# A diffusion transformer layer on one core: LayerNorm 1's scalars re-ranked, one room for two column sums, the last Newton steps on ScalarE

## The chip, the cores and the metric

One core of a Trainium2 chip runs the whole program. The time is device microseconds of one launch, from the core's first instruction to its last, with the launch's own small part around it. Before the change three executions took 1171.78, 1173.62 and 1175.6 us; the median is 1173.62 us. One more execution was profiled, and all views come from that one.

The engines are named as in the profile: PE (TensorE, the matrix products; PEld are its weight loads), DVE (VectorE), ACT (ScalarE), POOL (GpSimd) and SP (SyncE, whose queue issues all the loads here).

## What is computed

One layer with an adaptive modulation: six vectors (shift, scale and gate, twice) come from a conditioning vector; attention over 256 latent and 256 context tokens; an output projection; a gated residual; a LayerNorm; a modulated SwiGLU feed-forward part; a gated residual; a second LayerNorm. Everything is float32, D = 2048 columns, 5632 hidden columns.

```python
def layer_norm(x, g, b):
    xf = x.astype(jnp.float32)
    mu = jnp.mean(xf, axis=-1, keepdims=True)
    var = jnp.mean(jnp.square(xf - mu), axis=-1, keepdims=True)
    return ((xf - mu) * lax.rsqrt(var + EPS) * g + b).astype(x.dtype)
...
        sh1, sc1, g1, sh2, sc2, g2 = ada_mods(c, w_ada[layer], b_ada[layer])
...
        x = layer_norm(DN_ALPHA * x + g1 * (heads @ w_out[layer]), ln1_g[layer], ln1_b[layer])

        x = layer_norm(DN_ALPHA * x + g2 * swiglu(modulate(x, sh2, sc2), w_gate[layer], w_up[layer], w_down[layer]),
                       ln2_g[layer], ln2_b[layer])
```

## The kernel before

The 256 tokens are two tiles of 128 rows, t = 0 and 1. Every large product is done in three passes (`mm3`, lines 223 to 226): a float32 operand is split into a high part, cast by ACT (`hi`, L214 or L446), and a low part, the difference, by DVE (`lo`, L215 or L449); PE then adds hi by hi, lo by hi and hi by lo. A weight block of 512 x 512 is one load of 1 MB into a `raw` buffer (four of them), two ACT casts and two DVE casts of 128 x 1024 each, and 24 products of 512 columns (four slices of 128 rows, two tiles, three passes). The raw buffer is free again after its second DVE cast; there are four rooms for pairs of hi and lo.

The work runs in stages: the modulated input and its projection, attention, the output projection with the gated residual, LayerNorm 1, the first half of the gate and up products (`first_half`), the rest of the feed-forward part, the down projection, LayerNorm 2 and the store.

Up to LayerNorm 1 the order of the instructions on all five engines is written by a planner in the kernel, the class `Flow`. Each step is added with an engine, a duration in nanoseconds, the steps it comes after, the rooms it takes and gives, and a rank (`F.at`, in planned microseconds; smaller goes first among the steps that are ready). `Flow.run` plays the plan and issues the steps in the order that comes out. A step becomes ready some time after its forerunner ends: `SAME` on the same engine, `OTHER` across engines. END, the planned end of attention, is the base of the ranks around LayerNorm 1.

The output projection takes its column blocks n = 0 to 3 (`flow_out`, 512 columns each). The last one is done tile by tile: all products of tile 0, then all of tile 1. Behind each block DVE multiplies by the gate (L1035), adds to the residual (L1038, L1041) and takes statistics (`bn_stats`, L1044). When the four blocks of a tile are through, `ln_scalars(t)` (L969 to L979) makes mean and 1/sqrt(var + eps): an aggregation, four small steps that set up a start value from the bits of the variance, and three Newton rounds of two steps. `normalise(n, t)` (L986) then subtracts and scales 512 columns. `scalars(t)` (L1226 on) is `ln_scalars` with `normalise` of block 0.

Behind the planner the order is still as written until `region.__exit__`, and the compiler's scheduler places the rest. `z_flip` (L1233) transposes two column slices of a tile on PE; `z_rest` (L1338 to L1341) modulates them on ACT and splits them into `u2h` and `u2l`; `first_products(i, t)` are the twelve products of a tile with the first block of w_gate (i = 0) or w_up (i = 1). Before the change the written order is: z_rest of tile 0, scalars of tile 1, gate products of tile 0, z_flip of tile 1, up products of tile 0, z_rest of tile 1, then all products of tile 1, then the six late `normalise`.

The modulation of the feed-forward part needs, for each of four column groups, a sum over w_ada. Group 1's shift is summed by PE (`m1_sums`, L1200: 16 products into `bank1`), copied by ACT into `adav1` and turned into columns by four small products (`second_shifts`, L1213). Group 1's scale is summed by DVE (L332, sixteen steps over four loads of 1 MB; `scales`, an `ada_vector_steps`), into a room that POOL zeroes first (L309) and to which a short bias load goes (L315); `second_scales` (L1221) makes columns of it. `vector_sums` gives the one room with the tag `adav`; `late_sums[1]` gives a different one, with the tag `lgb`. Groups 2 and 3 (`side`) follow in the same way, summing shift and scale together, in `adav` and `lgb`. The scale steps are merged with three weight blocks of `first_half`.

At the end, behind the last block of the down projection, DVE does per tile the residual (L962, L963), the statistics (L964), `ln_scalars`, four steps that subtract the mean and multiply by g (L1447) and four that multiply by 1/sigma and add b (L1448), each followed by a store.

Of the kernel before, what the change touches and what calls it, by code (L numbers as in the profile page):

```python
# [12 lines left out]
F32 = mybir.dt.float32  # L13
F32R = mybir.dt.float32r
BF16 = mybir.dt.bfloat16
I32 = mybir.dt.int32
ET = mybir.EngineType
AF = mybir.ActivationFunctionType
ALU = mybir.AluOpType
# [3 lines left out]
P = 128  # L23
D = 2048
# [11 lines left out]
NB = 512  # L36
# [29 lines left out]
class Flow:  # L66
# [1 line left out]


    ENGINES = ("SP", "PE", "ACT", "DVE", "POOL")  # L70
    SAME = {"SP": 0, "PE": 0, "ACT": 60, "DVE": 80, "POOL": 80}
    OTHER = {"SP": 2000, "PE": 270, "ACT": 90, "DVE": 90, "POOL": 150}

    PATIENCE = 0
# [75 lines left out]
def dit_layer(ctx: ExitStack, tc: tile.TileContext, x, c, cx, c_ctx, w_ada, b_ada, w_in, q_norm_g,  # L150
              k_norm_g, sink_logit, w_out, ln1_g, ln1_b, w_gate, w_up, w_down, ln2_g, ln2_b,
              rope_cos, rope_sin, out):
    nc = tc.nc
# [134 lines left out]
    def ada_vector_steps(starts, width, sums, done):  # L288


        st = {}
        ns = len(starts)
        w = ns * width
        nk = G4 * NB // w

        def step(g):
            if g == 0:
                st["a"] = first_sums(sums(), starts, width)
            raw = raw_tile()
            vector_load(raw, starts, width, g)  # L300
            for i in range(G4 * NB // min(w, 2 * NB)):
                vector_sum(raw, st["a"], w, g, i)
            if g == KD // nk - 1:
                done(st["a"])

        return [lambda g=g: step(g) for g in range(KD // nk)]
# [29 lines left out]
    def vector_sums(width):  # L336
        return main.tile([P, 2 * NB], F32, tag="adav", name="adav")[:, :width]
# [625 lines left out]
        nc.vector.tensor_add(base[:, t, sl], base[:, t, sl], y)  # L963
        nc.vector.bn_stats(stats[:, t, n, :], base[:, t, sl])  # L964

    def ln_scalars(t):

        mv = main.tile([P, 2], F32, tag="mv", name="mv", bufs=2)
        nc.vector.bn_aggr(mv, stats[:, t, :, :])  # L969
        v = main.tile([P, 2], F32, tag="lv", name="lv", bufs=2)  # L970
        y = main.tile([P, 1], F32, tag="ly", name="ly", bufs=2)
        a = main.tile([P, 1], F32, tag="la", name="la", bufs=2)
        nc.vector.tensor_scalar_add(v[:, 0:1], mv[:, 1:2], EPS)
        nc.vector.tensor_single_scalar(a.bitcast(I32), v[:, 0:1].bitcast(I32), 1, op=ALU.logical_shift_right)
        nc.vector.tensor_scalar_mul(v[:, 1:2], v[:, 0:1], -0.5)
        nc.vector.tensor_scalar(y.bitcast(I32), a.bitcast(I32), -1.0, float(0x5F3759DF), op0=ALU.mult, op1=ALU.add)
        for _ in range(3):
            nc.vector.tensor_scalar(a, y, y, v[:, 1:2], op0=ALU.mult, op1=ALU.mult)
            nc.vector.tensor_scalar(y, a, 1.5, y, op0=ALU.add, op1=ALU.mult)  # L979
        return mv[:, 0:1], y  # L980

    norm = {}

    def normalise(n, t):
# [225 lines left out]
    def second_shifts(sb):  # L1210
        ps = wk_bank()
        for j in range(4):
            nc.tensor.matmul(ps[:, 4 * j : 4 * j + 4], lhsT=sb[:, j * P : (j + 1) * P], rhs=sel, start=True, stop=True)  # L1213
        pv = ps[:, 0:16].rearrange("p (j i s) -> p j i s", i=2, s=2)
        bs = bcol[:, 3 * KD + 4 : 3 * KD + 8, None].to_broadcast([P, 4, 2])
        nc.vector.tensor_tensor(sh2[:, 4:8, :], pv[:, :, 0, :], bs, op=ALU.add)
# [9 lines left out]
    def scalars(t):  # L1226
        norm[t] = ln_scalars(t)
        normalise(0, t)
# [8 lines left out]
    F.at = END + 50  # L1237
    first_gate = flow_weights(w_gate, 0, G4, 0, NB, W)
    first_up = flow_weights(w_up, 0, G4, 0, NB, W)
    F.at = END + 33  # L1240
    a = F.add("DVE", 3300, lambda: scalars(0), [outs[n, 0] for n in range(4)])
    zroom = [Buf("wk"), Buf("wk")]
    for i in range(2):
# [82 lines left out]

            first_half += [lambda g=g, step=step: step(g) for g in range(groups[f])]
    late_sums = [lambda: vector_sums(2 * NB), lambda: pb.tile([P, 2 * NB], F32, tag="lgb", name="adav")]
    scales = ada_vector_steps((4 * D + NB,), NB, lambda: late_sums[1]()[:, :NB], second_scales)
    side = sum((second_modulation(g, late_sums[g - EARLY_G]) for g in range(EARLY_G, ng)), [])  # L1330

    def z_rest(t, kk):
# [9 lines left out]

    firsts = [[acc_bank() for _ in range(NT)] for _ in range(2)]

    def first_products(i, t):
        ps = firsts[i][t]
        tt = slice(t * P, (t + 1) * P)
        for j in range(4):
            hl = (first_gate, first_up)[i][j // 2][0]
            c = slice((j % 2) * NB, (j % 2 + 1) * NB)  # L1350
            mm3(ps, u2h[:, j, tt], u2l[:, j, tt], (hl.hi[:, c], hl.lo[:, c]), j == 0, j == 3)

    for kk in (0, 2):
        z_rest(0, kk)
    scalars(1)
    first_products(0, 0)
    for kk in (0, 2):
        z_flip(1, kk)
    first_products(1, 0)
    for kk in (0, 2):  # L1360
        z_rest(1, kk)
    adav1 = vector_sums(NB)
    nc.scalar.copy(adav1, bank1.t)
    for i in range(2):
        first_products(i, 1)
    for i in range(2):
# [3 lines left out]
        for t in range(NT):  # L1370
            normalise(n, t)
    region.__exit__(None, None, None)
    second_shifts(adav1)
    run(merge(first_half[2 : 2 * ONE_F - 1], scales))
    combine(1)
    z_part(4)
# [64 lines left out]
        run(merge(steps, side))  # L1441

    for t in range(NT):
        mu, rstd = ln_scalars(t)
        for n in range(4):
            sl = slice(n * NB, (n + 1) * NB)
            nc.vector.scalar_tensor_tensor(xt[:, t, sl], xt[:, t, sl], mu, l2g[:, sl], op0=ALU.subtract, op1=ALU.mult)  # L1447
            nc.vector.scalar_tensor_tensor(xt[:, t, sl], xt[:, t, sl], rstd, l2b[:, sl], op0=ALU.mult, op1=ALU.add)  # L1448
            nc.sync.dma_start(out[0, t * P : (t + 1) * P, sl], xt[:, t, sl])
# [48 lines left out]
```

## Time and profile before

| | us |
|---|---|
| median of three executions | 1173.62 (1171.78 to 1175.6) |
| the profiled execution | 1172.63 |
| its span, first to last instruction | 1170.9 |
| PE busy | 1144.9 |
| DVE busy | 822.3 |
| ACT busy | 537.5 |
| POOL busy | 25.5 |

The profiled execution's time lies 1.73 us above its span, and about 1 us below the median of the others. In a row of the timeline the columns are the start, the duration, the engine, the line, the operation, what it writes and reads, how many instructions are merged, and in brackets the idle time before it and what ended that. In a row of the groups they are the line, engine, operation, operands and count, then busy time and the mean of one in ns, then the idle time before them. In a row of stages each engine has its busy time within the stage. A row of loads has the source, the size and, as its last number, the time from issue to landing. In the chain of work that ended last each piece has its start and length.

### The profile page before, as it was taken

To read this page: it belongs to the slowest core of one execution; us is meant where nothing else is said; L and a number is where in the kernel's file an instruction comes from. 1 tells how busy PE (TensorE), PEld (TensorE's weight loads), DVE (VectorE), ACT (ScalarE), POOL (GpSimd) and SP (SyncE) were. 2 spreads that over 40 slices of the span, in tenths; PEclk is the share of its full clock that TensorE was granted. 3 is DMA by queue.
4 is the path that set the end of the run, shared out by engine and by line. 5 is a ranking of instruction groups with operands and counts; after the bars stand their busy time and mean duration, and the time that the engine had idled before them with its cause. 6 is when DMAs were issued, how large, how long until landed. Compare 5 with 4: busy or idle time off the path is not lost.

```text
span 1170.9 us, 14367 instructions
## 1 busy us (share of the span) xinstructions
PE 1144.9 (98%) x5563; PEld 928.6 (79%) x5563; DVE 822.3 (70%) x1064; ACT 537.5 (46%) x760; POOL 25.5 (2%) x44
## 2 busy tenths in 40 slices
PE   8999999999999989999999999999999999999995
PEld 8767588888887778888888888888888788888884
DVE  4763588888899887766767566665665777676556
ACT  3341542777776255545454444444444433433440
POOL 1000030000000000000000000000000000000000
PEclk9999999999999999999999999999999999999997
DMA  8999988526587678889957555555556898877531
GB/s 266 390 403 397 357 360 287 181 72 215 182 290 280 225 271 320 302 293 316 322 194 239 182 189 196 188 180 180 184 198 212 299 330 317 283 257 256 192 132 73
DMA packets 150716, 292.95 MB, mean 250 GB/s; under 512 B 5580, under 2 KB 20332, under 8 KB 148343
## 3 DMA queue, kind: packets, MB, share of 16 engines
q1 hardware_dynamic: 150648, 292.04, 71.4%
q8 instruction: 44, 0.72, 0.2%
q14 instruction: 24, 0.20, 0.0%
HBM read 289.92 MB, written 2.10 MB: 249 GB/s over the span
## 4 chain that ended last, share of the span: by engine, by line
PE 93%; DVE 4%; DMA 2%; ACT 1%; issue 0%; SPq 0%; DVEq 0%; ACTq 0%
PE acc L224 27%; PE acc L225 27%; PE acc L226 27%; PE wk L865 2%; PE wk L485 2%; PE acc L1070 1%; PE wk L854 1%; PE wk L1304 1%; PE wk L224 1%; PE wk L226 1%; PE wk L225 1%; PE wk L342 1%; DMA lgb<-in_ln_b_dram 1%; PE wk L572 1%; DVE adav L332 1%; DVE lo L215 0%
## 5 line engine op out<-in xcount | busy, mean ns | idle before, releaser
L215 DVE TENSOR_TENSOR lo<-raw,hi 128x1024 fp32r<-128x1024 f32 x258 | 313.8, 1223 | 206.0 <-ACT hi L214 202.6
L214 ACT CAST hi<-raw 128x1024 fp32r<-128x1024 f32 x258 | 271.1, 1055 | 353.0 <-PE acc L226 331.3
L224 PE MATMUL acc<-hi,u2h 128*128 128x512 f32 x704 | 275.5, 391 | 1.2 <-ACT u2h L1340 1.2
L225 PE MATMUL acc<-lo,u2h 128*128 128x512 f32 x704 | 274.2, 389 | 0.8 <-DVE lo L215 0.8
L226 PE MATMUL acc<-hi,u2l 128*128 128x512 f32 x704 | 274.1, 389 | 0.0
L225 PEld LDWEIGHTS acc<-lo,u2h 128*128 128x128 f32 x704 | 132.2, 188 | 28.4 <-DVE lo L215 1.6
L224 PEld LDWEIGHTS acc<-hi,u2h 128*128 128x128 f32 x704 | 132.2, 188 | 28.2 <-ACT u2h L1340 1.4
L226 PEld LDWEIGHTS acc<-hi,u2l 128*128 128x128 f32 x704 | 132.2, 188 | 27.7 <-DVE u2l L1341 0.2
L446 ACT CAST hi<-raw 128x1024 fp32r<-128x1024 f32 (+1 forms) x86 | 87.9, 1033 | 135.3 <-PE acc L226 68.9
L224 PE MATMUL acc<-hi,hTh 128*128 128x512 f32 x344 | 135.5, 394 | 0.0
L226 PE MATMUL acc<-hi,hTl 128*128 128x512 f32 x344 | 134.0, 390 | 0.0
L225 PE MATMUL acc<-lo,hTh 128*128 128x512 f32 x344 | 134.0, 389 | 0.0
L332 DVE SCALAR_TENSOR_TENSOR adav<-raw,cs,adav 128x512 f32<-128x512 f32 (+1 forms) x128 | 121.4, 948 | 9.0 <-DMA raw<-in_w_ada_dram 7.2
L449 DVE TENSOR_TENSOR lo<-raw,hi 128x1024 fp32r<-128x1024 f32 (+1 forms) x86 | 102.5, 1198 | 28.0 <-ACT hi L446 27.7
L224 PE MATMUL acc<-hi,uh 128*128 128x512 f32 x256 | 102.8, 402 | 1.0 <-ACT hi L446 1.0
L225 PE MATMUL acc<-lo,uh 128*128 128x512 f32 x256 | 100.2, 391 | 1.1 <-DVE lo L449 1.1
L226 PE MATMUL acc<-hi,ul 128*128 128x512 f32 x256 | 99.9, 390 | 0.0
L225 PEld LDWEIGHTS acc<-lo,hTh 128*128 128x128 f32 x344 | 64.6, 188 | 14.4 <-issue 1.0
L224 PEld LDWEIGHTS acc<-hi,hTh 128*128 128x128 f32 x344 | 64.6, 188 | 14.1 <-issue 1.0
L226 PEld LDWEIGHTS acc<-hi,hTl 128*128 128x128 f32 x344 | 64.6, 188 | 13.4
L224 PEld LDWEIGHTS acc<-hi,uh 128*128 128x128 f32 x256 | 48.1, 188 | 17.7 <-issue 4.6
L225 PEld LDWEIGHTS acc<-lo,uh 128*128 128x128 f32 x256 | 48.1, 188 | 11.0 <-DVE lo L449 2.0
(201 smaller groups left out, 1166.8 us busy)
## 6 DMA issues: line engine op xcount, KB each, us to landing
raw<-in_w_ada_dram SPq DMA_DIRECT2D x72, 1024.0 KB, 7.0
raw<-in_w_gate_dram SPq DMA_DIRECT2D x44, 1024.0 KB, 5.2
raw<-in_w_up_dram SPq DMA_DIRECT2D x44, 1024.0 KB, 5.1
raw<-in_w_down_dram SPq DMA_DIRECT2D x44, 1024.0 KB, 5.6
raw<-in_w_ada_dram SPq DMA_DIRECT2D x48, 512.0 KB, 4.9
raw<-in_w_in_dram SPq DMA_DIRECT2D x18, 1024.0 KB, 8.0
raw<-in_w_out_dram SPq DMA_DIRECT2D x16, 1024.0 KB, 4.9
raw<-in_w_in_dram SPq DMA_DIRECT2D x10, 512.0 KB, 8.2
```

The source lines that it names most:

```text
L214: nc.scalar.copy(hi[:, :n], raw[:, s : s + n])
L215: nc.vector.tensor_tensor(lo[:, :n], raw[:, s : s + n], hi[:, :n].bitcast(F32), op=ALU.subtract)
L224: nc.tensor.matmul(ps, lhsT=xh, rhs=w[0], start=first, stop=False)
L225: nc.tensor.matmul(ps, lhsT=xh, rhs=w[1], start=False, stop=False)
L226: nc.tensor.matmul(ps, lhsT=xl, rhs=w[0], start=False, stop=last)
L332: nc.vector.scalar_tensor_tensor(a[:, c : c + piece], raw[:, f : f + piece], cs[:, g * (G4 * NB // w) + j, 2:3], a[:, c : c + piece], op0= ...
L342: nc.tensor.matmul(ps, lhsT=ones, rhs=sb[:, s : s + NB], start=True, stop=True)
L446: nc.scalar.copy(hl.hi[:, :n], raw.t[:, s : s + n])
L449: nc.vector.tensor_tensor(hl.lo[:, :n], raw.t[:, s : s + n], hl.hi[:, :n].bitcast(F32), op=ALU.subtract)
L485: nc.tensor.matmul(bank.t[32 * j : 32 * j + 32, :width], lhsT=cs[:, k, 2 - 2 * i : 34 - 2 * i], rhs=raw.t[:, c * width : (c + 1) * width], ...
L572: nc.tensor.transpose(ps.t[:, (j * 2 + t) * P : (j * 2 + t + 1) * P], src, ident)
L865: nc.tensor.matmul(o_ps.t[:, : 2 * P], lhsT=v, rhs=pT.t[:, k].rearrange("p h q -> p (h q)"), start=k == 0, stop=k == 3)
```

## The change

Six edits:

- `SAME["DVE"]`, the time that the planner lets pass between two dependent DVE steps, goes from 80 ns to 0.
- The rank of the first tile's `scalars(0)` goes from END + 33 to END + 20. (The casts of the first w_gate and w_up blocks keep END + 50, the last projection block ranks around END + 33.)
- The products of tile 0 with w_up are split: two of the four slices before the second tile's transposes, two behind them.
- The copy of the shift sum (`adav1`) moves ahead of the first products, and `second_shifts` from behind the late `normalise` to ahead of the second tile's `z_rest`.
- The scale sum of group 1 (`scales`) goes into the room `adav`, the one in which the shift sum `adav1` lies, instead of `lgb`.
- In the last LayerNorm the Newton rounds run on ACT: a Square, an Identity with the scale and the bias read from tiles (the bias is a new constant tile `half3` of 1.5, filled by POOL), and a Copy with the scale read from a tile, three times per tile. In all LayerNorms the start value is written before the factor -0.5 instead of behind it.

```diff
-    SAME = {"SP": 0, "PE": 0, "ACT": 60, "DVE": 80, "POOL": 80}
+    SAME = {"SP": 0, "PE": 0, "ACT": 60, "DVE": 0, "POOL": 80}
...
-    def ln_scalars(t):
+    def ln_scalars(t, beside=False):
...
+        nc.vector.tensor_scalar(y.bitcast(I32), a.bitcast(I32), -1.0, float(0x5F3759DF), op0=ALU.mult, op1=ALU.add)
         nc.vector.tensor_scalar_mul(v[:, 1:2], v[:, 0:1], -0.5)
-        nc.vector.tensor_scalar(y.bitcast(I32), a.bitcast(I32), -1.0, float(0x5F3759DF), op0=ALU.mult, op1=ALU.add)
         for _ in range(3):
-            nc.vector.tensor_scalar(a, y, y, v[:, 1:2], op0=ALU.mult, op1=ALU.mult)
-            nc.vector.tensor_scalar(y, a, 1.5, y, op0=ALU.add, op1=ALU.mult)
+            if beside:
+                nc.scalar.activation(a, y, AF.Square)
+                nc.scalar.activation(a, a, AF.Identity, bias=half3, scale=v[:, 1:2])
+                nc.scalar.activation(y, y, AF.Copy, scale=a)
+            else:
+                nc.vector.tensor_scalar(a, y, y, v[:, 1:2], op0=ALU.mult, op1=ALU.mult)
+                nc.vector.tensor_scalar(y, a, 1.5, y, op0=ALU.add, op1=ALU.mult)
         return mv[:, 0:1], y
 
+    half3 = main.tile([P, 1], F32, tag="half3", name="half3")
+    nc.gpsimd.memset(half3, 1.5)
...
-    F.at = END + 33
+    F.at = END + 20
     a = F.add("DVE", 3300, lambda: scalars(0), [outs[n, 0] for n in range(4)])
...
-    scales = ada_vector_steps((4 * D + NB,), NB, lambda: late_sums[1]()[:, :NB], second_scales)
+    scales = ada_vector_steps((4 * D + NB,), NB, lambda: vector_sums(NB), second_scales)
...
-    def first_products(i, t):
+    def first_products(i, t, js=range(4)):
         ps = firsts[i][t]
         tt = slice(t * P, (t + 1) * P)
-        for j in range(4):
+        for j in js:
...
     scalars(1)
+    adav1 = vector_sums(NB)
+    nc.scalar.copy(adav1, bank1.t)
     first_products(0, 0)
+    first_products(1, 0, (0, 1))
     for kk in (0, 2):
         z_flip(1, kk)
-    first_products(1, 0)
+    first_products(1, 0, (2, 3))
+    second_shifts(adav1)
     for kk in (0, 2):
         z_rest(1, kk)
-    adav1 = vector_sums(NB)
-    nc.scalar.copy(adav1, bank1.t)
...
-    second_shifts(adav1)
...
-        mu, rstd = ln_scalars(t)
+        mu, rstd = ln_scalars(t, True)
```

## The prediction

> **What bounds the kernel now.** I read the page first (busy times and the chain of work that ended last), then busy time by stages, then the timeline around LayerNorm 1 and at the end.
>
> ```profile
> span 1170.9 us, 14367 instructions
> PE 1144.9 (98%) x5563; PEld 928.6 (79%) x5563; DVE 822.3 (70%) x1064; ACT 537.5 (46%) x760; POOL 25.5 (2%) x44
> PE 93%; DVE 4%; DMA 2%; ACT 1%; issue 0%; SPq 0%; DVEq 0%; ACTq 0%
> ```
>
> PE is busy for 98% of the span and makes 93% of the last chain. So a change gains only where PE is idle: 26 us in all, 14.6 of it behind the last product (below).
>
> ```profile
> core 0: us, PE busy (x) PEld busy (x) DVE busy (x) ACT busy (x) POOL busy (x), PEclk, DMA share, GB/s
> 150.00:405.00 255.00, 254.17 (x1221) 207.88 (x1223) 226.65 (x367) 149.38 (x294) 13.01 (x19) 1.00 0.66 232
> 405.00:427.00 22.00, 17.90 (x102) 12.48 (x95) 20.05 (x49) 11.09 (x21) 1.48 (x2) 1.00 0.58 193
> 427.00:450.00 23.00, 23.00 (x110) 19.02 (x109) 16.91 (x20) 12.22 (x19) 1.74 (x4) 1.00 0.97 361
> ```
>
> The change touches three places. In 150 to 405 us (attention and output projection, the planner's part) PE idles for only 0.83 us. In 405 to 427 us (LayerNorm 1) it idles for 4.1 us, and DVE is busy 91%. Right behind, the DMA share is 0.97. The 4.1 us in detail:
>
> ```profile
> 403.17 0.68 DVE L1044 BATCH_NORM_STATS2 stats<-xt 128x6 f32<-128x512 f32 x1
> 404.76 3.64 PE L1200 MATMUL wk<-raw,cs 128*32 128x512 f32 x32
> 404.87 0.69 DVE L1035 TENSOR_TENSOR oacc<-acc,g1b 128x512 f32<-128x512 f32 x1 [1.01 <-PE acc L226]
> 408.01 0.55 DVE L986 TENSOR_SCALAR xt<-xt,mv,ly 128x512 f32<-128x512 f32 x1
> 408.61 0.66 PE L1233 MATMUL wk<-ident,xt 128*128 128x128 f32 x4 [0.21 <-DVE xt L986]
> 409.14 0.81 ACT L1338 ACTIVATE uf<-wk,mB,mA 128x128 f32<-128x128 f32 x2 [14.10 <-PE wk L1233]
> 409.98 0.41 ACT L1340 CAST u2h<-uf 128x256 fp32r<-128x256 f32 x1
> 410.43 0.50 PE L224 MATMUL acc<-hi,u2h 128*128 128x512 f32 x1 [1.17 <-ACT u2h L1340]
> 414.06 0.75 DVE L332 SCALAR_TENSOR_TENSOR adav<-raw,cs,adav 128x512 f32<-128x512 f32 x1
> 416.20 0.63 PE L1233 MATMUL wk<-ident,xt 128*128 128x128 f32 x4 [2.72 <-DVE xt L986]
> 419.54 2.82 DVE L986 TENSOR_SCALAR xt<-xt,mv,ly 128x512 f32<-128x512 f32 x6
> ...
> 425.02 0.79 PE wk L1213 x8
> 442.29 0.79 PE wk L1221 x8
> ```
>
> All rows but the last two are the timeline; those two are the chain in order of time. PE waits 0.21 and 1.17 us for the first tile's normalised columns and their casts, then 2.72 us for the second tile's scalars. After that it runs unbroken: products and column shifts done at 425.81 us (425.02 + 0.79), three blocks of 24 products, then the column scales at 442.29. That is PE's pace: 72 products in 16.48 us, 0.229 each, 5.49 a block.
>
> **The change, term 1: LayerNorm 1, the lead.** The order of instructions in the changed program, read without times, shows DVE doing the first tile's scalars and its first `normalise` directly behind that tile's last statistics, ahead of the second tile's L1035; two casts of w_up move behind. In the old order DVE reached those statistics at 403.2 us with two casts in between (1.22 us each by the form of L215 below), so the scalars can start near 401.5 and end with the normalise near 404.6 (408.56 before). PE's 16 sums are split: eight, the flips, eight. Eight take 1.82 us (half of 3.64), so the flips stand at 406.6 instead of 408.6, and the other eight end at 408.9 over the casts, which took 410.39 - 408.61 = 1.8 us. On DVE the second tile's three steps (404.9 to 407.0) and the two w_up casts (to 409.3) now precede the first u2l, which costs PE some 0.4 us. Then 12 + 6 products (4.1 us, to 413.4) cover the second tile's scalars and normalise (3.1 us, 410.1 to 413.2): the 2.72 us wait goes. Flips, six products, shifts, 24 products: PE is where it was at 425.81 by about 421.7. The lead is 4.1 us, all of the idle time.
>
> **Term 2: what the shared room takes back.** Before, the scale sums had a room of their own and five of their sixteen L332 ran from 414.06, before the six late `normalise` of 419.54: in DVE's free time. Now the sum lies in the room of the shift sum. It can't be zeroed before PE has read that (near 416.0), and in DVE's new order all sixteen stand behind the six `normalise`, first one at a time with a weight cast (L215) after each, then eight in a row, then four.
>
> ```profile
> L332 DVE SCALAR_TENSOR_TENSOR adav<-raw,cs,adav 128x512 f32<-128x512 f32 x80 | 59.9, 749 | 8.6 <-DMA raw<-in_w_ada_dram 7.2
> L214 ACT CAST hi<-raw 128x1024 fp32r<-128x1024 f32 x258 | 271.1, 1055 | 353.0 <-PE acc L226 331.3 <-issue 10.6 <-DMA raw<-in_w_down_dram 8.7
> L215 DVE TENSOR_TENSOR lo<-raw,hi 128x1024 fp32r<-128x1024 f32 x258 | 313.8, 1223 | 206.0 <-ACT hi L214 202.6
> ...
> raw<-in_w_ada_dram SPq DMA_DIRECT2D x1, 1024.0 KB, 5.0
> ...
> raw<-in_w_gate_dram SPq DMA_DIRECT2D x1, 1024.0 KB, 5.1
> ...
> raw<-in_w_ada_dram SPq DMA_DIRECT2D x1, 1024.0 KB, 6.5
> ```
>
> (The groups by form; then the loads issued at 417.53, 424.97 and 426.11 us.) From 419.8 us a pair of L332 and L215 costs about 1.8 us on DVE (0.75 + 1.22 less their overlap). The fourth L332 ends near 425.9 and gives back the first load's buffer, so the third w_ada load is issued at 426.0, not 417.53, and SP's queue holds the next gate block's load behind it. It lands 5 us later, at 431.0; the gate load 2.5 us behind (424.97 + 5.1 and 426.11 + 6.5 lie 2.5 apart), at 433.4. PE has finished its two blocks at 421.7 + 11.0 = 432.7. The gate's high cast (1.05 us) ends at 434.4, its low cast at 435.6; PE has done one product, so it stands 2.7 us. It reaches the column scales at 440.9 instead of 442.29. DVE's last four L332 (to 439.8) and ACT are not later. Kept: **-1.3 us**. From below, -4.1 if nothing is given back. From above: the loads one more transfer (2.5 us) late is +1.2, and a little more where the next columns wait for the scales.
>
> The moved shifts (0.79 us) are the same work earlier. The one new memset of `half3` lies on POOL at the start, off the chain.
>
> **Term 3: the planner's zero.** `SAME["DVE"]` = 0 reorders the attention and projection: dependent DVE steps stand back to back.
>
> ```profile
> 388.54 1.28 DVE L1035 TENSOR_TENSOR oacc<-oacc,g1b 128x512 f32<-128x512 f32 x2
> 392.63 0.69 DVE L1032 TENSOR_TENSOR oacc<-oacc,acc 128x512 f32<-128x512 f32 x1 [1.60 <-PE acc L226]
> ...
> 1148.17 0.69 DVE L962 TENSOR_TENSOR yt<-acc,g2sb 128x512 f32<-128x512 f32 x1 [5.85 <-PE acc L226]
> 1148.90 0.69 DVE L963 TENSOR_TENSOR xt<-xt,yt 128x512 f32<-128x512 f32 x1
> ```
>
> Independent steps follow each other after 0.60 us (two in 1.28), dependent ones after 0.73. I count some 16 more dependent neighbours before the scalars: +2.1 us of DVE, against 1.60 us of waiting at 392.63 that the two gate casts now fill, and two casts less before the scalars. Cover: counted with the same durations, the low casts of the output weights lie about 10 us ahead of their products in either order, and with that gone each 0.1 us would count. PE's own order changes too: counting 0.23 us a product, it has 4.6 to 9.4 us of work between a pair of heads' last score and the first flip of its probabilities, where it had 5.2 to 12.7. The tightest before did not stall. I take **+0.3 us**: below -0.8 (all idle gone), above +5.1 (rival below).
>
> **Term 4: Newton on ScalarE.** Six DVE steps become nine ACT steps per tile. DVE still makes the start value at the same place.
>
> ```profile
> 1152.17 0.15 DVE L976 TENSOR_SCALAR ly<-la 128x1 int32<-128x1 int32 x1
> 1155.10 2.08 DVE L1448 SCALAR_TENSOR_TENSOR xt<-xt,ly,l 128x512 f32<-128x512 f32 x3
> 1155.91 0.39 PE L226 MATMUL acc<-hilo,hTl 128*128 128x512 f32 x1
> 1157.09 0.68 DVE L962 TENSOR_TENSOR yt<-acc,g2sb 128x512 f32<-128x512 f32 x1
> 1164.54 2.74 DVE L1448 SCALAR_TENSOR_TENSOR xt<-xt,ly,l 128x512 f32<-128x512 f32 x4
> ...
> L841 ACT ACTIVATE es<-es 128x2 f32<-128x2 f32 x8 | 1.6, 200 | 0.0
> L859 ACT COPY pT<-wk 128x512 f32<-128x512 f32 x32 | 17.7, 590 | 2.5 <-PE wk L854 2.1
> L849 ACT ACTIVATE pr<-pr,ll 128x512 f32<-128x512 f32 x32 | 21.5, 722 | 1.0 <-DVE rs_t L243 0.7 <-DVE ll L846 0.2
> L1338 ACT ACTIVATE uf<-wk,mB,mA 128x128 f32<-128x128 f32 x8 | 3.2, 452 | 19.2 <-PE wk L1233 19.2
> ```
>
> An ACT step of almost no columns costs 0.20 us; 0.76 ns a column (590 against 200). A scale read from a tile adds 0.13 (722 against 590), scale and bias 0.16 (452 against 0.30 for 128 columns). Square 0.20, Identity 0.36, Copy 0.33, each 0.03 after the one it needs (409.14 + 0.81 to 409.98): 0.98 us a round, 2.94 for three. Starting at 1152.32 + 0.05 they end at 1155.31: L1448 at 1155.34, 0.24 late. The second tile's L962 stands behind three of these, so it is 0.24 late, and loses 0.24 again: **+0.5 us**. DVE's six steps cost 0.5 us less but DVE only waits for it. Below, every step at 0.20: 2.07 us a tile, -1.3 in all. Above, at 0.45 a step: 4.3 us, +3.2.
>
> The Trainium skill (ScalarE: Activation LUTs, What ACT_TABLE_LOAD costs) gives 186 ns plus about 93 ns for each operand read from a tile; estimated from that a round is 0.84 us. It also says that ACTIVATEs back to back overlap by 93 ns, and with that the nine would take 1.7 us. By that the time would be the fourth rival's. The rows of L1338 and L1340 show 0.03 us between dependent steps, no overlap.
>
> **Sum.** -1.3 + 0.3 + 0.5 = -0.5 us on the profiled execution's own 1172.63, so 1172.1. The median of the runs (1173.62) is 1.0 above that execution: **1173.1 us**.
>
> **The rivals.**
> 1. *The lead is kept.* For it: DVE has gaps, and the third load need not hold the gate's. Against it: DMA share 0.97 there. -4.1 + 0.3 + 0.5 = -3.3, with the attention's idle gone too -4.4: 1169.2 to 1170.3.
> 2. *Slower: PE waits at the flips of attention.* A pair's chain is 0.69 (maximum) + 2 x 0.98 (powers) + 0.72 (weighing) + small steps, about 3.9 us, and any cast of 1.05 or 1.22 us standing between lengthens it. From 5.4 us on the new order stalls. At 6.5 us the gaps of 4.6, 5.4, 5.4, 6.0, 6.2 and 6.3 lose 1.9 + 1.1 + 1.1 + 0.5 + 0.3 + 0.2 = 5.1. Against it: the old order had 5.2, 5.4 and 6.0 too and idled 0.83. With the rest: +4.3, 1177.9.
> 3. *The shared room eats more than the lead*, one transfer later and again at the next columns: term 2 +1.8, 1176.2.
> 4. *Short ACT steps overlap* even when dependent (1.7 us a tile): L1448 1.0 earlier; the second L962 only 0.75, to PE's end at 1156.3; then 1.0 again. -1.7 for +0.5: 1170.9.
>
> **How the numbers follow.** Forecast 0.45, rivals 0.17, 0.18, 0.10, 0.10. About 0.3% (3.5 us) is what a measurement of this kernel can tell from no change. Faster by more: most of rival 1, some of 4, 0.17. Slower by more: rival 2, part of 3 and the tail's upper end, 0.22. The rest, 0.61. The range of 1169.2 to 1177.5 takes in both sides; the forecast's own is 1171 to 1175.5.
>
> **What would show it.** Right: PE idle in 405 to 427 us near 0.5 instead of 4.1; no 2.7 us wait at the second flips; the third w_ada load issued after 424; a new PE wait of 1 to 4 us for a low cast near 433; ACT's nine steps 2.5 to 3.2 us a tile. Wrong: waits of PE at L854 or L865 over 2 us in all (rival 2), no wait near 433 (rival 1), ACT's nine under 2.2 us (rival 4).

## The result and the profile after

The changed kernel takes 1176.58 us (median of 8 runs, 1176.42 to 1177.58) against 1173.34 us (8 runs, 1171.78 to 1175.60) for the kernel before: ratio 1.0030, 95% interval 1.0019 to 1.0041. It is slower by some 3 us. That is inside the predicted range, but a ratio of 1 (no change) lies outside the interval, and the forecast was 0.5 us faster, with no measurable change as its likeliest case. The profiled execution of the changed kernel (1177.55 us) lies 1 us above that median.

The page of the profile after:

```profile
span 1175.7 us, 14365 instructions
PE 1148.4 (98%) x5563; PEld 928.7 (79%) x5563; DVE 823.8 (70%) x1052; ACT 542.8 (46%) x778; POOL 25.7 (2%) x45
PE 85%; DMA 6%; DVE 5%; ACT 2%; issue 1%; SPq 0%; POOL 0%; DVEq 0%; ACTq 0%; POOLq 0%
```

PE is still busy 98%, but the last chain runs over DMA for 6% of the span instead of 2%. Busy time by stages, before and after (columns as in the prediction: each engine's busy us with instructions, granted PE clock, DMA share, GB/s):

```profile
30.00:100.00 70.00, 70.00 (x485) 49.43 (x484) 43.90 (x64) 23.98 (x38) 0.00 (x0) 1.00 1.05 396
100.00:150.00 50.00, 48.28 (x280) 32.72 (x279) 22.81 (x30) 19.97 (x30) 0.00 (x0) 1.00 0.96 363
```

```profile
30.00:100.00 70.00, 67.95 (x462) 48.45 (x465) 43.85 (x65) 25.14 (x40) 0.00 (x0) 1.00 1.06 380
100.00:150.00 50.00, 47.43 (x271) 29.61 (x263) 19.10 (x27) 15.26 (x23) 0.00 (x0) 0.97 1.02 373
405.00:427.00 22.00, 20.75 (x113) 14.09 (x112) 16.73 (x45) 7.08 (x16) 1.48 (x2) 1.00 0.42 145
427.00:450.00 23.00, 22.04 (x106) 18.19 (x105) 20.94 (x26) 11.42 (x16) 2.20 (x4) 1.00 0.77 274
450.00:500.00 50.00, 49.22 (x216) 40.12 (x216) 37.47 (x33) 27.08 (x35) 0.19 (x1) 1.00 0.96 342
```

LayerNorm 1 did most of what was forecast: PE's idle time in 405 to 427 us fell from 4.10 to 1.25 us. The loss lies where the change was to do nothing, in the first 150 us: the same transfers run at 380 instead of 396 GB/s with the DMA share as full as before, and PE, which never stood in 30 to 100 us before, idles for 2.05 us there. The instructions of the modulation sums L485 (durations in ns, then first and last start in us), before and after, and two of PE's waits of the first 160 us after (total us, times, longest; before it was 0.8 us for L449 and none for L485):

```profile
L485 PE MATMUL wk<-raw,cs x384: 272/498/618, 11.3 to 143.0; 128*32 128x512 f32 x96, 128*32 128x128 f32 x64, 128*32 128x256 f32 x32
```

```profile
L485 PE MATMUL wk<-raw,cs x384: 272/498/617, 10.7 to 149.1; 128*32 128x512 f32 x96, 128*32 128x128 f32 x64, 128*32 128x256 f32 x32
```

```profile
PE acc L225 <- DVE lo L449: 2.2, 3, 0.8
PE wk L485 <- DMA raw<-in_w_ada_dram: 1.2, 2, 0.8
```

The last sum starts 6.1 us late. If all of its 143 us had gone by the rate, that would be 143 x (396/380 - 1) = 6.0 us, but the rate does not account for all of it. In this execution the granted PE clock also fell to one half for 3.4 us, which by itself costs up to 1.7 us; before had no such drop there. The rows of the drop and of 120 to 150 us after, then 120 to 150 us of raw32, an experiment below with the same low rate and no drop:

```profile
133.60:137.00 3.40, 3.40 (x10) 2.66 (x9) 2.30 (x3) 1.66 (x3) 0.00 (x0) 0.50 1.04 382
120.00:150.00 30.00, 28.28 (x166) 16.97 (x165) 13.65 (x20) 13.27 (x21) 0.00 (x0) 0.94 1.01 365
```

```profile
120.00:150.00 30.00, 28.10 (x171) 16.69 (x170) 14.42 (x20) 13.26 (x21) 0.00 (x0) 1.00 1.00 364
```

Over the 18 profiled kernels, where the clock is 1.00 in 120 to 150 us, the last L485 starts at 142.3 to 143.9 us at the high rate and at 147.2 to 147.6 at the low one. So the low rate costs about 4.5 us there, and the rest of the 6.1 goes with the clock.

Where the offset to the kernel before is won and lost, from the first and last starts of single lines in each kernel's trace (us; the line numbers are those of before, in other kernels the same statements):

| | last L485 | first L918 | first L1200 | first L1221 | last L1304 | span |
|---|---|---|---|---|---|---|
| before | 143.0 | 386.5 | 404.8 | 442.1 | 914.1 | 1170.9 |
| after | 149.1 | 389.7 | 410.6 | 446.7 | 919.1 | 1175.7 |
| pad32 | 148.8 | 392.2 | 410.5 | 447.9 | 919.9 | 1176.1 |
| after_fill | 143.9 | 384.5 | 405.5 | 441.6 | 913.9 | 1170.5 |
| same0 | 145.2 | 385.8 | 406.8 | 447.4 | 920.0 | 1176.7 |
| fill_room | 142.3 | 382.8 | 403.8 | 443.7 | 916.5 | 1173.0 |

After against before: +6.1 at the start, +5.8 at LayerNorm 1, +5.0 at the end of the second modulation, +4.8 at the end. (The other rows belong to the experiments.)

### The profile page after: what moved, and what is told of

It reads as the page before. It is cut to its first block, busy times and chain, and to the rows that moved or that the text cites. A ratio compares the mean times of both kernels' runs of the same rounds, so it can differ in the third digit from the quotient of the medians.

```text
span 1175.7 us, 14365 instructions
## 1 busy us (share of the span) xinstructions
PE 1148.4 (98%) x5563; PEld 928.7 (79%) x5563; DVE 823.8 (70%) x1052; ACT 542.8 (46%) x778; POOL 25.7 (2%) x45
## 4 chain that ended last, share of the span: by engine, by line
PE 85%; DMA 6%; DVE 5%; ACT 2%; issue 1%; SPq 0%; POOL 0%; DVEq 0%; ACTq 0%; POOLq 0%
PE acc L225 25%; PE acc L226 25%; PE acc L224 25%; DMA raw<-in_w_in_dram 3%; PE wk L865 2%; DMA raw<-in_w_ada_dram 1%; PE wk L854 1%; PE wk L485 1%; DVE adav L332 1%; PE wk L1311 1%; DVE lo L215 1%; DVE lo L449 1%; PE wk L224 1%; PE wk L342 1%; PE wk L226 1%
## 5 line engine op out<-in xcount | busy, mean ns | idle before, releaser
L224 PE MATMUL acc<-hi,u2h 128*128 128x512 f32 x704 | 274.9, 391 | 1.1 <-ACT u2h L1347 0.8
L226 PE MATMUL acc<-hi,u2l 128*128 128x512 f32 x704 | 274.2, 389 | 0.0
L224 PEld LDWEIGHTS acc<-hi,u2h 128*128 128x128 f32 x704 | 132.1, 188 | 29.2 <-ACT u2h L1347 1.8
L226 PEld LDWEIGHTS acc<-hi,u2l 128*128 128x128 f32 x704 | 132.1, 188 | 28.1 <-DVE u2l L1348 0.6
L224 PE MATMUL acc<-hi,hTh 128*128 128x512 f32 x344 | 135.4, 394 | 0.0
L226 PE MATMUL acc<-hi,hTl 128*128 128x512 f32 x344 | 133.9, 389 | 0.0
L332 DVE SCALAR_TENSOR_TENSOR adav<-raw,cs,adav 128x512 f32<-128x512 f32 (+1 forms) x128 | 121.4, 948 | 12.3 <-DMA raw<-in_w_ada_dram 10.2
L449 DVE TENSOR_TENSOR lo<-raw,hi 128x1024 fp32r<-128x1024 f32 (+1 forms) x86 | 101.7, 1196 | 34.3 <-ACT hi L446 33.8
L224 PE MATMUL acc<-hi,uh 128*128 128x512 f32 x256 | 103.7, 405 | 1.6 <-ACT hi L446 1.0
L226 PE MATMUL acc<-hi,ul 128*128 128x512 f32 x256 | 100.6, 393 | 0.0
L224 PEld LDWEIGHTS acc<-hi,hTh 128*128 128x128 f32 x344 | 64.6, 188 | 14.2 <-issue 1.0
L226 PEld LDWEIGHTS acc<-hi,hTl 128*128 128x128 f32 x344 | 64.6, 188 | 13.3
L224 PEld LDWEIGHTS acc<-hi,uh 128*128 128x128 f32 x256 | 48.5, 190 | 19.9 <-ACT hi L446 4.6
```

What stands on the lines that cost most here:

```text
L224: nc.tensor.matmul(ps, lhsT=xh, rhs=w[0], start=first, stop=False)
L226: nc.tensor.matmul(ps, lhsT=xl, rhs=w[0], start=False, stop=last)
L332: nc.vector.scalar_tensor_tensor(a[:, c : c + piece], raw[:, f : f + piece], cs[:, g * (G4 * NB // w) + j, 2:3], a[:, c : c + piece], op0= ...
L449: nc.vector.tensor_tensor(hl.lo[:, :n], raw.t[:, s : s + n], hl.hi[:, :n].bitcast(F32), op=ALU.subtract)
```

## The experiments

**What the new tile moves.** In the compiled program `half3`, four bytes a partition, takes 32, and all tiles allocated behind it move. The four weight buffers `raw` begin at byte 26,624 of each partition before (52 x 512), at 26,656 after. The kernel before has a line that sets this place, 416 unused bytes behind `ident`, which the diff leaves as it was. First four kernels, three of them to tell address from order:

pad32 is the kernel before with

```
+    half3 = main.tile([P, 1], F32, tag="half3", name="half3")
+    nc.gpsimd.memset(half3, 1.5)
```

> The kernel before with nothing added but the tile half3 (one float a partition) and its memset, which nobody reads. In the compiled program the four weight buffers raw then begin at byte 26,656 of each partition instead of 26,624, and everything allocated behind half3 moves by 32 bytes with them. Theory A (address): transfers into buffers that start 32 bytes past a multiple of 64 are slower, as the profile after has it (385 to 387 GB/s in slices of 40 to 110 us, where before had 401 to 405); the last modulation product L485 ends near 149 us instead of 143, and the time is 4 to 6 us above the kernel before, about 1178. Rival B (order): the 6 us lost before 150 us come from the other edits, so this kernel stays within 1 us of the kernel before, at 401 to 405 GB/s. Rival C (chip to chip): the rate differs by chip, then this kernel and the kernel before agree on one chip.

1177.88 us against 1173.44, ratio 1.0039 (1.0026 to 1.0053). That is theory A: the tile alone, read by nobody, costs as much as the whole change.

after64 is the changed kernel with `main.tile([P, 16], ...)` and `bias=half3[:, 0:1]`.

> The changed kernel with half3 widened from 1 to 16 floats a partition (the first is used), which puts the raw buffers at byte 26,688, a multiple of 64 again; every engine's order is that of the changed kernel. Theory A (address): the start is as fast as before (about 405 GB/s, L485 ends near 143 us), and the time falls by 4 to 6 us from the changed kernel's 1176.6 to 1171 to 1172.5, below the kernel before. Rival B (order): 1176 to 1177 as the changed kernel. If 64 bytes are not enough and a larger multiple counts (before had a multiple of 512): between the two.

1177.10, ratio 1.0033 (1.0021 to 1.0046). A multiple of 64 bytes isn't enough; the DMA rate in 30 to 100 us is 380 GB/s again.

after_dve is the changed kernel with `ln_scalars(t)` for `ln_scalars(t, True)` at the end, and without `half3`.

> The changed kernel with the last LayerNorm's Newton steps on VectorE as before, and without half3, so that the raw buffers are at byte 26,624 as before. Theory A: 1171 to 1172, the start at 405 GB/s and 0.2 to 0.5 us less than the changed kernel with aligned buffers (nine ScalarE steps of about 2.9 us a tile, late by 0.24 us each). Rival B (order): the loss at the start stays, 1176. Rival D: the Newton steps on ScalarE are the main cost at the end, then this one is more than 1.5 us below the changed kernel with half3 widened.

1172.07, ratio 0.9990 (0.9981 to 0.9998). The rest of the change is a small gain.

same0 is the kernel before with

```
-    SAME = {"SP": 0, "PE": 0, "ACT": 60, "DVE": 80, "POOL": 80}
+    SAME = {"SP": 0, "PE": 0, "ACT": 60, "DVE": 0, "POOL": 80}
```

> The kernel before with VectorE's same-engine delay in the planner set to 0 and nothing else: the attention and projection part is ordered anew, the rest and all addresses stay. Theory A with the prediction's term 3: +0.3 us, within -0.8 to +1.5 of the kernel before. Rival B (order): most of the loss, +3 to +5 us. The prediction's second rival (TensorE waits at the attention flips): +5 us with waits of TensorE at L854 and L865 of over 2 us.

1178.11, ratio 1.0039 (1.0026 to 1.0051): slower, against theory A's own number. It is not the attention. In the table the offset goes from +2.2 at the start to +2.0 at L1200, and then jumps to +5.3 at L1221. PE's waits in 400 to 520 us, before and in same0:

```profile
PE wk L1233 <- DVE xt L986: 2.9, 2, 2.7
PE acc L224 <- ACT u2h L1340: 1.2, 1, 1.2
```

```profile
PE wk L1233 <- DVE xt L986: 4.9, 1, 4.9
PE acc L224 <- ACT u2h L1340: 0.8, 1, 0.8
```

The second tile's flips wait 4.9 us instead of 2.7. The start's +2.2 is no finding: over the kernels with `raw` and the activations of the first phases on multiples of 256 bytes the last L485 ranged from 142.3 to 145.2, and the four from 144.5 up, same0 among them, are those with a clock of 0.94 in 120 to 150 us.

**Which tiles, and what grain.** after_fill is the changed kernel with

```
-    fill(main, 416)
+    fill(main, 384)
```

so that `raw` is back at 26,624. raw32 moves `raw` alone (half3 ahead of it, 480 unused bytes behind), hilo32 everything behind `raw` by 32 bytes, pad256 and pad128 everything from `raw` on by 256 and 128.

> The changed kernel with the unused bytes behind ident cut from 416 to 384, so that half3 fits ahead of the raw buffers and they begin at byte 26,624 as before (xt and the small tiles between lie 32 bytes earlier; the steps on ScalarE and every order stay those of the changed kernel). Theory A (address of raw and what lies behind it): the start is as before (L485 ends near 143 us, 394 to 396 GB/s in 30 to 100 us) and the time is 1171.5 to 1172.5, as the variant without half3 had it (1172.07). Rival E (Newton's steps on ScalarE or the two together are the loss): 1176 to 1177. If the place of xt counts too, between.

> The kernel before with half3 and its memset (unused) ahead of the raw buffers and 480 unused bytes behind them: raw moved to byte 26,656, the cast halves hi and lo and all behind at multiples of 512 as before (512 bytes further on). Theory A1 (the place that a transfer writes to counts): as slow as with everything moved, 1177 to 1178.5, at 380 GB/s in 30 to 100 us. Theory A2 (what TensorE, ScalarE and VectorE read and write behind raw counts): 1173 to 1174, at 395 GB/s.

> The kernel before with 32 unused bytes behind the raw buffers: raw stays at byte 26,624, hi, lo and all behind lie 32 bytes past a multiple of 512. Theory A1 (the place that a transfer writes to counts): 1173 to 1174, as before, 394 to 396 GB/s in 30 to 100 us. Theory A2 (operands of the engines): 1177 to 1178.

> The kernel before with half3 of 64 floats (unused): raw begins at byte 26,880, a multiple of 256 but not of 512. If 256 bytes are the grain: 1173 to 1174 at 395 GB/s in 30 to 100 us. If 512 are: 1177 to 1178 at 380 GB/s.

> The kernel before with half3 of 32 floats (unused): raw begins at byte 26,752, a multiple of 128 but not of 256. If 256 bytes are the grain for transfers: 1177 to 1178.5 and 380 GB/s in 30 to 100 us, as 32 and 64 had. If 128 are: 1173 to 1174.5 and 395 GB/s.

| kernel | raw begins at | median us | ratio to before (95%) |
|---|---|---|---|
| after_fill | 26,624 | 1171.60 | 0.9972 (0.9962 to 0.9982) |
| raw32 | 26,656 | 1178.47 | 1.0029 (1.0020 to 1.0039) |
| hilo32 | 26,624 | 1174.27 | 0.9998 (0.9988 to 1.0007) |
| pad128 | 26,752 | 1179.50 | 1.0043 (1.0030 to 1.0056) |
| pad256 | 26,880 | 1174.07 | 0.9994 (0.9985 to 1.0003) |

Their stage of 30 to 100 us, in the order of the table:

```profile
30.00:100.00 70.00, 69.86 (x482) 49.04 (x481) 44.13 (x65) 25.12 (x39) 0.00 (x0) 1.00 1.05 395
```

```profile
30.00:100.00 70.00, 67.80 (x462) 48.49 (x465) 44.16 (x65) 25.88 (x41) 0.00 (x0) 1.00 1.05 381
```

```profile
30.00:100.00 70.00, 69.87 (x484) 49.21 (x483) 43.92 (x65) 24.33 (x39) 0.00 (x0) 1.00 1.06 396
```

```profile
30.00:100.00 70.00, 67.59 (x458) 48.35 (x461) 43.79 (x65) 25.14 (x39) 0.00 (x0) 1.00 1.06 380
```

```profile
30.00:100.00 70.00, 70.00 (x484) 49.42 (x483) 44.15 (x65) 24.58 (x39) 0.00 (x0) 1.00 1.05 397
```

395 to 397 GB/s where `raw` begins on a multiple of 256, 380 or 381 where it is 32 or 128 off (after64: 64 off, 380), whatever else moved. Over all 18 kernels it is 388 to 398 for the thirteen with `raw` on a multiple of 256. It is the place that a load writes to (raw32 slow, hilo32 not), and 256 bytes are the grain: 128 off is slow, 256 off is not. The engines read `raw` too, but the products L485 that read it take 498 ns in the median in before, in after_fill and in raw32, while the packets of the loads themselves take longer (last section). The Trainium skill (DMA: Bandwidth & Descriptors, How a descriptor splits into AXI transactions) tells of 256-byte transactions that must start on a 256-byte boundary, so that a piece off the boundary can take more of them. It says so of reading and gives no rate; the runs agree with its grain, for the address written.

**The three other parts, each undone in after_fill.** fill_room gives the column scales their own room again, fill_same80 puts VectorE's delay back, fill_dve the Newton steps:

```
-    scales = ada_vector_steps((4 * D + NB,), NB, lambda: vector_sums(NB), second_scales)
+    scales = ada_vector_steps((4 * D + NB,), NB, lambda: late_sums[1]()[:, :NB], second_scales)
```

```
-    SAME = {"SP": 0, "PE": 0, "ACT": 60, "DVE": 0, "POOL": 80}
+    SAME = {"SP": 0, "PE": 0, "ACT": 60, "DVE": 80, "POOL": 80}
```

```
-        mu, rstd = ln_scalars(t, True)
+        mu, rstd = ln_scalars(t)
```

> The changed kernel with 32 unused bytes less, so that raw is at byte 26,624 (the variant of that name had 1171.6), and with the column scales back in the room lgb they had before, the rest of LayerNorm 1 as changed. The prediction's term 2 says that the shared room gives back 2.8 us of the lead: then TensorE idles 0.5 us or less in 427 to 500 us (1.7 in the variant with the shared room), the scales come 2 to 3 us earlier, and the time is 1168.8 to 1170. Rival (the shared room costs little, TensorE waits there for casts in any case): 1171.2 to 1172.

1177.38 us (1174.75 to 1181.57), ratio 1.0034 (1.0021 to 1.0047): the other way round. It is 5.8 us above after_fill by the medians, and in the profiles it takes 4.3 us more from the first L1200 to the last L1304 (512.7 against 508.4). The profiled execution, 1174.9 us, is one of its fastest, so the 4.3 us need not be all. VectorE's timeline of fill_room at the second tile's scalars, then that of after_fill:

```profile
410.47 0.26 DVE L969 BATCH_NORM_AGGREGATE mv<-stats 128x2 f32<-128x24 f32 x1
411.33 0.75 DVE L332 SCALAR_TENSOR_TENSOR adav<-raw,cs,adav 128x512 f32<-128x512 f32 x1
412.00 0.27 DVE L983 TENSOR_SCALAR la<-ly,lv 128x1 f32<-128x1 f32 x1
412.18 0.74 DVE L332 SCALAR_TENSOR_TENSOR adav<-raw,cs,adav 128x512 f32<-128x512 f32 x1
412.84 0.21 DVE L984 TENSOR_SCALAR ly<-la,ly 128x1 f32<-128x1 f32 x1
...
416.89 0.54 DVE L993 TENSOR_SCALAR xt<-xt,mv,ly 128x512 f32<-128x512 f32 x1
```

```profile
412.15 0.26 DVE L969 BATCH_NORM_AGGREGATE mv<-stats 128x2 f32<-128x24 f32 x1
...
413.07 0.27 DVE L983 TENSOR_SCALAR la<-ly,lv 128x1 f32<-128x1 f32 x1
413.38 0.21 DVE L984 TENSOR_SCALAR ly<-la,ly 128x1 f32<-128x1 f32 x1
413.63 0.27 DVE L983 TENSOR_SCALAR la<-ly,lv 128x1 f32<-128x1 f32 x1
...
414.75 0.55 DVE L993 TENSOR_SCALAR xt<-xt,mv,ly 128x512 f32<-128x512 f32 x1
```

With a room of its own the scale sum's L332 are free to run, and the schedule puts seven of them, 0.74 us each, between the scalars' little steps. From the aggregate to the first `normalise` it is 6.42 us (416.89 - 410.47) instead of 2.60. The flips, which start on that `normalise`:

```profile
417.58 1.09 PE L1240 MATMUL wk<-ident,xt 128*128 128x128 f32 x4 [4.19 <-DVE xt L993]
```

```profile
415.44 0.63 PE L1240 MATMUL wk<-ident,xt 128*128 128x128 f32 x4 [0.39 <-DVE xt L993]
```

4.19 us of waiting against 0.39. same0 has the same picture (its six L332 stand between the steps, where before had two). Whether the own room costs as much with the planner's delay at 80, as in before, was not tried on the changed order.

> The changed kernel with raw at byte 26,624 and VectorE's same-engine delay in the planner back at 80. The prediction's term 3 (delay 0 costs 0.3): 1171.3, within 0.8 of the variant with delay 0 (1171.6). If the delay of 0 is a loss by itself, as the kernel before with it alone had it (1178.1 against 1173.4), and the other edits hide only part of it: 1168 to 1170. If the delay of 0 and the new order of LayerNorm 1 only pay together: 1173 to 1176, with TensorE idle 3 us or more in 405 to 427 us.

1172.66, ratio 0.9996 (0.9986 to 1.0006). So within the changed kernel a delay of 0 costs nothing, while alone it cost 4.7 us. It may be worth 1 us (by the medians) to 2.8 (by the ratio of after_fill, 0.9972), but that gain is not shown: the intervals of fill_dve (below) and after_dve, which have the delay of 0 as well, overlap that of fill_same80.

> The changed kernel with raw at byte 26,624, half3 kept, and the Newton steps of the last LayerNorm on VectorE as before. The prediction's term 4 (0.24 us later a tile on ScalarE, 0.5 in all): 1171.1, at most 1.3 below or 0.3 above the variant with ScalarE's steps (1171.6). If ScalarE's short steps overlap (the prediction's rival of that kind): 1 to 3 us above it.

1171.36, ratio 0.9981 (0.9972 to 0.9991): not to be told from after_fill (0.9962 to 0.9982). The time from the last L1304 to the end in the profiles doesn't tell either: 256.1 us in fill_dve (912.7 to 1168.8) and 256.6 in after_fill, but 256.8 in before, which has these steps on VectorE too.

**The two extra weight buffers** of the first phases lie 96 bytes past a multiple of 256 in the kernel before (byte 212,320) and in after_fill. fill_araw is after_fill with 160 unused bytes more ahead of them; since activations lie behind those bytes too, it moved two things. araw_only moves the two buffers alone by 160, acts_only the activations alone by 160, acts256 both by 256.

> The changed kernel with raw at byte 26,624, and with 160 unused bytes more ahead of the two extra weight buffers of the first phase, which before had at byte 212,320 (96 past a multiple of 256); now 212,480, a multiple of 512. If a transfer's write address costs by its place in 256 bytes, the loads into these two (a part of the loads of the first 150 us) get faster too: the DMA rate in 30 to 100 us rises above 395 GB/s, up to 400 to 405, L485 ends 1 to 2 us earlier, and the time falls by 1 to 2 us to 1169.5 to 1170.5. If only raw counts: 1171 to 1172.

> The changed kernel with raw at byte 26,624 (1171.6) and 160 unused bytes directly ahead of the two extra weight buffers, which alone move, to byte 212,480, a multiple of 512 (before 96 past a multiple of 256). If the address costs a transfer into these as into raw: the DMA rate in 30 to 100 us rises above 395 GB/s, up to 405, and the time falls by 1 to 2 us, to 1169.5 to 1170.6. If what bounds the phase is not these buffers: 1171 to 1172. If moving these two was the loss of the kernel with both moved: 1178.

> The changed kernel with raw at byte 26,624, and the activations of the first two phases (accumulators, transposed tokens, queries, keys and so on) 160 bytes further on, no longer at multiples of 256; the two extra weight buffers 512 bytes further on, as far off a multiple of 256 as before. If TensorE's operands are slower there: 1177 to 1179, products of 512 columns in the first 300 us at a mean of 398 to 409 ns instead of 390 to 401, nothing lost after 390 us. If not: 1171 to 1172.

> The changed kernel with raw at byte 26,624, and the activations and the two extra weight buffers 256 bytes further on. If a move by a whole 256 bytes is harmless for TensorE's operands: 1171 to 1172. If it is their distance from the weight halves that counts: 1177 to 1179.

fill_araw took 1178.83 (ratio 1.0046, 1.0030 to 1.0062), araw_only 1171.61 (0.9981, 0.9973 to 0.9990), acts_only 1178.30 (1.0031, 1.0019 to 1.0044), acts256 1171.47 (0.9976, 0.9968 to 0.9985). Bringing the two buffers to an even address gains nothing that shows; moving the activations was the loss. The groups of PE in the first 300 us, in acts_only and in acts256 (busy us, mean ns):

```profile
L224 PE MATMUL acc<-hi,uh 128*128 128x512 f32 x256 | 104.8, 410 | 1.0 <-ACT hi L447 1.0
L226 PE MATMUL acc<-hi,ul 128*128 128x512 f32 x256 | 101.9, 398 | 0.0
```

```profile
L224 PE MATMUL acc<-hi,uh 128*128 128x512 f32 x256 | 102.6, 401 | 1.0 <-ACT hi L446 1.0
L226 PE MATMUL acc<-hi,ul 128*128 128x512 f32 x256 | 99.9, 390 | 0.0
```

Part of this is the clock, 0.94 in 120 to 150 us of acts_only and 1.00 in acts256. In 150 to 300 us, with a clock of 1.00 in both, the means are 406 against 398 ns (L224) and 395 against 390 (L226): a product takes 1 to 2% longer with `uh` and `ul` off by 160 bytes and `hi` and `lo` in place.

## Why the prediction was wrong, point by point

- **The step that failed** is the cost of the new tile: "The one new memset of `half3` lies on POOL at the start, off the chain." The memset is free, the tile isn't. It moves the weight buffers off a 256-byte boundary, for some 4.5 of the 6.1 us at the start in the profile (the rest goes with the clock), and 3.4 to 5.0 us of the time by the ratios of the three kernels that put `raw` off it without the rest of the change (raw32, pad32, pad128). Taking 32 bytes out ahead of `raw` turns the changed kernel from 1176.58 to 1171.60.
- **What bounds the kernel** was read from 150 us on. In 30 to 100 us both are full before: PE 70.00 of 70 us, DMA share 1.05. There a slower load costs at once (PE idles for 2.05 us). Whether a faster one would gain isn't shown: in araw_only the rate didn't rise (397 GB/s).
- **Term 1, the lead of 4.1 us:** PE's idle time in 405 to 427 us was forecast near 0.5 and was 1.25, so the lead was 2.85 us (4.10 - 1.25). The 2.7 us wait at the second flips became 0.39, as in this timeline of after (the sums start 5.8 us later than in before):

```profile
410.64 1.92 PE L1207 MATMUL wk<-raw,cs 128*32 128x512 f32 x16
412.50 0.66 PE L1240 MATMUL wk<-ident,xt 128*128 128x128 f32 x4
415.86 0.50 PE L224 MATMUL acc<-hi,u2h 128*128 128x512 f32 x1 [0.85 <-ACT u2h L1347]
420.62 0.63 PE L1240 MATMUL wk<-ident,xt 128*128 128x128 f32 x4 [0.39 <-DVE xt L993]
441.58 0.50 PE L225 MATMUL acc<-lo,u2h 128*128 128x512 f32 x1 [0.96 <-DVE lo L215]
```

- **Term 2, 2.8 us given back:** PE idles 1.74 us in 427 to 500 us of after where it had none, 0.96 of it the forecast wait for a low cast (last row above), which was to be 2.7 us; it ends at 441.6 for a forecast 435.6, and 5.8 us of the difference are the start's. The third w_ada load was forecast at 426.0, with the next gate block behind it; SP's queue in after_fill, which starts as early as before:

```profile
425.47 0.39 SPq L322 DMA_DIRECT2D raw<-in_w_ada_dram  x1
427.93 0.39 SPq L194 DMA_DIRECT2D raw<-in_w_gate_dram  x1
```

  Net from the first sum L1200 to the last L1304: 509.3 us before, 508.5 after, 508.4 in after_fill, so -0.8 to -0.9 for the forecast -1.3. That the net came out so near is partly luck, because the lead was 1.25 us too large and what it gives back 1.1 too large. The reading was wrong: the shared room was booked as a price paid for the lead, with -4.1 if nothing were given back. fill_room shows that in this order there is no lead at all without it (512.7 us); the sum that cannot start is what keeps VectorE free for the scalars. Rivals 1 and 3 both rested on that reading and did not come. The measured 1176.58 lies beside rival 3's 1176.2 by chance: term 2 didn't come out at +1.8.
- **Term 3, +0.3:** from the last L485 to L1200 it is 261.8 us before and 261.5 after, -0.3. Rival 2 did not come: neither L854 nor L865 is among PE's waits. What the term missed is that the delay acts on LayerNorm 1 as well: alone it cost 4.7 us, 3.3 of them in the profile between L1200 and L1221, and in the changed order it costs nothing.
- **Term 4, +0.5:** the nine steps of the second tile run from 1166.80 to 1169.70, 2.90 us for the forecast 2.94:

```profile
1166.80 0.20 ACT L979 ACTIVATE la<-ly 128x1 f32<-128x1 f32 x1 [6.72 <-DVE ly L975]
1167.03 0.39 ACT L980 ACTIVATE la<-la,half,lv 128x1 f32<-128x1 f32 x1
1167.45 0.29 ACT L981 ACTIVATE ly<-ly,la 128x1 f32<-128x1 f32 x1
...
1169.41 0.29 ACT L981 ACTIVATE ly<-ly,la 128x1 f32<-128x1 f32 x1
```

  Each step begins 0.03 us after the one it needs, so rival 4's overlap is absent. From the first tile's aggregation to the second tile's last four steps it is 14.18 us before (to the 1164.54 of the prediction's rows) and 14.58 after, 0.4 for the forecast 0.5. Before, then after:

```profile
1150.36 0.26 DVE L969 BATCH_NORM_AGGREGATE mv<-stats 128x2 f32<-128x24 f32 x1
```

```profile
1155.16 0.26 DVE L969 BATCH_NORM_AGGREGATE mv<-stats 128x2 f32<-128x24 f32 x1
...
1169.74 2.74 DVE L1456 SCALAR_TENSOR_TENSOR xt<-xt,ly,l 128x512 f32<-128x512 f32 x4 [1.66 <-ACT ly L981]
```

Without the 32 bytes the sum of -0.5 us would have had the right side and too small a size: after_fill's profiled span is 0.4 us below that of before, its median 2.7 us, most of which goes with the clock (last section).

## What to carry to other kernels

A new tile is a change to every address behind it: before costing it at nothing, list where the buffers that loads write to begin, before and after, and look for unused bytes that someone put there to set those places. A room, a buffer or a wait that looks like a price can be what holds other work out of the way; undo it alone before booking a gain for its removal. A planner's constant had no price of its own here, only one for each order of the work around it. Before putting a difference of two profiles down to one cause, look at the granted clock of both.

## What was not expected of the hardware

- The rate of loads falls by 4% (396 to 380 GB/s in 30 to 100 us) when their target is 32, 64 or 128 bytes off a multiple of 256. The transfers of 60 to 110 us, nearly all in packets of 2 KB (512 columns), before and then after:

```profile
DMA packets 10123, 20.02 MB, mean 400 GB/s; under 512 B 369, under 2 KB 369, under 8 KB 10119
```

```profile
DMA packets 9753, 19.29 MB, mean 386 GB/s; under 512 B 363, under 2 KB 363, under 8 KB 9748
```

  A sixteenth of 400 GB/s takes 81.9 ns for 2 KB, of 386 84.9. The traces also time each packet. In these 50 us one of 2 KB took 85.3 ns in the mean before and 88.4 after; in 30 to 44 us, where w_ada comes in pieces of 256 columns (1 KB), one of 1 KB took 47.0 and 50.9. So it is some 3 to 4 ns a row on each of the 16 engines, for both lengths. This shows where the queue is full: in 600 to 750 us, at 199 and 200 GB/s, the median packet of 2 KB takes 84 ns in both.
- Products whose `uh` and `ul` lie 160 bytes off, with `hi` and `lo` on a multiple of 512, take 1 to 2% longer (406 for 398 ns at a clock of 1.00). With both off by the same 32 (hilo32) or 128 bytes (pad128) the means of L224 in the first 300 us are 402 and 403, as in before (402). That points to the distance between them rather than the own place, but neither was tried by itself.
- The granted PE clock fell to one half for 3.4 us at a time, as in the row of after above; that is up to 1.7 us each time, or 0.92 over 22 us and 0.94 over 30. In 405 to 427 us it was 0.92 in both kernels in which PE waits 4.2 or 4.9 us there (fill_room, same0), in three of the six with a wait of 2.7 or 2.8 us (hilo32, raw32, pad128; 1.00 in before, pad32, pad256), and 1.00 in the ten in which no wait is over 1.2 us. But the length of a wait doesn't settle it: in 120 to 150 us the clock was 0.94 in eight of the 18 kernels (after, pad32, same0, pad256, fill_same80, fill_araw, araw_only, acts_only) and 1.00 in the others, and in all of them the longest wait of PE there is 1.0 us. What decides was not tested. The Trainium skill (TensorE: Matmul & The Clock Gate, What's actually happening) has the clock fall after an idle window of about 3.4 us; here it also fell beside shorter waits.
- The clock differs between executions of one kernel, and the time goes with it. Of the 29 executions of the kernel before that were timed beside after_fill, nine had a mean clock of 0.992 and a median of 1176.1 us, fourteen 0.994 and 1174.2, three 0.995 and 1172.3. Eight of the nine of after_fill had 0.995, with a median of 1171.6. So most of the 2.7 us between the two medians goes with the clock, which fits the 0.4 us between the two profiles, neither of which had a drop ahead of the last product. That after_fill keeps its clock because its 2.7 us wait is gone was not tested by itself.
